# Decoded tokens next to the chain over chunks, a group's end in a lane of its own, and operations held back in program order

## The chip, the core and the metric

The kernel runs on one core of one Trainium2 chip. A core has five engines with queues of their own: TensorE (PE, with its weight loads shown as PEld), VectorE (DVE), ScalarE (ACT), GpSimd (POOL) and SyncE (SP), which here only issues transfers. The metric is the device time of one execution in microseconds (us), as a median over runs. Before the change it is 1681.28 us (three runs, 1680.93 to 1681.66).

## What is computed

One trunk layer of a hybrid causal decoder, for 256 prompt tokens and for 8 sequences of 4 decoded tokens each. All weights and states are in float32. Cut to what matters, the reference is

```python
h = rmsnorm(x, norm_pre_mix)
z = h @ w_in                                   # 2048 -> 3360 + 1024 + 2048 + 2048
zs, zp, zga, zgb = split(z)
ya, new_wkv  = rwkv7(zs + (prev(zs) - zs) * mu_shift, state_wkv, ...)   # 16 heads of 64
yb, new_pool = pool(zp, state_pool, ...)       # causal means over 2, 4, 8, 16 tokens
m = sigmoid(zga) * (ya @ w_branch_a) + sigmoid(zgb) * (yb @ w_branch_b)
x = x + rmsnorm(m @ w_out, norm_post_mix)
f, new_conv = conv_ffn(rmsnorm(x, norm_pre_ffn), state_conv, ...)       # 2048 -> 2 x 5632 -> 2048
x = x + rmsnorm(f, norm_post_ffn)
```

and the recurrence within `rwkv7`, for each head and token, with a matrix state `s` of 64 x 64:

```python
sa = s @ a_t
s = s * w_t[None, :] + outer(sa, b_t) + outer(v_t, k_t)
y_t = s @ r_t
```

followed by a normalisation of `y` over each head, a bonus term and a gate `g`.

## The kernel before, in words

**Layout.** Channels lie on the 128 partitions and the 288 tokens (256 prompt tokens and 32 decoded ones, `N`) along the free dimension. Each product of the layer goes by tiles of 128 output channels: `dense` runs over 16 (or 8, or up to 16) tiles of 128 input channels and sums them in one PSUM bank of 128 x 288.

**Weights in two parts.** Every float32 weight is split into a high part `whi` (a cast on ScalarE, L196) and the rest `wlo` (a subtraction on VectorE, L197), and every input likewise, so that three matmuls (`three`, L254 to L256) stand for one float32 product. Weights come in *units* of four input tiles (128 x 512 elements, 256 KB): `load_to` issues the load of a unit on SP, `split_to` its two casts. `take(u)` casts three units ahead and loads nine ahead. One unit is twelve dense matmuls.

**Lanes.** The side work (everything of the recurrence, the norms) is written as generators in lanes. At the end of each unit `advance` runs the operations put off by `defer` and steps each lane once, so a `yield` in a generator is a slot of one unit. `yield 2` is two slots, `yield lambda: ...` waits until the condition holds. `drain_side` steps the lanes without any dense work until they are empty.

**Order.** The mixer runs in the order of `ORDER`: r, k and v of head group 0 (two heads' tiles, 4 heads); the eight tiles of the pooling branch with `pool_product`s; group 1; 16 products of branch b; group 2; 6 gates for b; group 3; 10 gates for b; 15 gates for a. Then come the 16 products of branch a (`seq_ba`), `w_out`, and the feed-forward part in three thirds. From the end of group 0's r, k and v to the first product of branch a there are 264 units.

**One head group.** `rkv(g)` makes r, k, v and puts `front(g)` into lane 1 and `late(g)` into lane 2.

- `front(g)`: decay, its running product, and the operands `AR` and `KB` of the chunked form; it sets `ready[g]`. Then the bonus `bv`.
- `late(g)`: the products `ps_g` of 64-token chunks (L625) and their masked copy `Gm`; the transposes `ps_t` into `BK`; `ps_v` into `UV`; the diagonal 32 x 32 blocks of `Gm` go through DRAM (`dA`) into `Ab`. Then two generators step together, one step of each per slot: `inverse`, 31 pairs of a multiplication and a sum on VectorE (L782, L785) that solve the 32 x 32 triangular blocks, and `sample`, the decoded tokens: `ps_sg` (L707 to L715), five dependent steps `ps_sl` (L743) and VectorE `UVs` (L745), and the state update `ps_st` (L765). The inverse goes through DRAM (`dW`) into `W`; `dve.transpose` makes `tq` (L827), `ps_q` (L833) and `ps_w` (L845) complete the 64 x 64 inverse. Then the chain over the four chunks, three slots a chunk: `ps_x`, a copy `X`; `ps_u`, the scaling into `UV`; `ps_s` and `ps_y`, the new state `S` and the copy into `Yt` (L900). Last the end of the group: the head norm, `ps_yt` (L926), the gate products `ps_gate` (L937) and `ya`, eight tiles in all for four groups, which branch a reads.

`late(g + 1)` can only begin when `late(g)` is through, since they share lane 2. The scratch `inv` of the inverse lies in a pool (`k2`) whose memory is the pooling stage's until that is over, so group 0 waits for it (`yield lambda: k2`).

**Who orders what.** The kernel is built with a planner: it takes the instructions of each engine in the order in which they were written, but lets one that its own timing thinks ready pass others that it thinks are not. On the chip each engine runs its list in that order and waits at each instruction for its inputs. `tc.keep_in_program_order(i)` (`pin`) ties an instruction behind the one that was written last before it on its engine.

## Time and profile before

| what | before |
|---|---|
| median of three runs | 1681.28 us |
| the profiled execution | 1685.43 us |
| span of its instructions | 1683.4 us |
| mean granted TensorE clock | 0.991 |
| PE, DVE, ACT, POOL busy | 97%, 66%, 48%, 22% |
| weights and states read from HBM | 262.67 MB |

The page of the profile covers one execution. A row of its groups of instructions reads: line, engine, operation, output <- inputs, shape, count, then busy time in us and the mean of one in ns, then the idle time of the engine just before them and what ended it. Matmuls are pipelined: a row of one shows 0.29 us though the next begins 0.13 us after it, so the rate is read from starts, not from durations.

The stages by time, from the first and last products of each: the start to 77 us (norm, the low-rank columns, group 0), the mixer from 77 to 662 us, branch a from 661.6 to 712.4 us, `w_out` to about 815 us, the second norm to about 835 us, and the feed-forward part to 1667 us.

### The profile page before, as it was taken

How to read it: one execution, taken by the hardware profiler on the slowest of the kernel's cores; microseconds unless marked ns; L12 is line 12 of the kernel's file. 1: busy time of each engine (PE TensorE's matmuls, PEld its weight loads, DVE VectorE, ACT ScalarE, POOL GpSimd, SP SyncE). 2: the span in 40 equal slices, each digit the busy share in tenths (PEclk: the TensorE clock that was granted, in tenths of full speed). 3: DMA queues.
4: the chain of work that ended last, by engine and by line, in shares of the span. 5: the costliest groups of instructions: out<-in, count | busy, mean ns of one | idle time of the engine just before them, and what ended most of it. 6: DMA issues, size and time to landing. Idle time of an engine off the chain costs nothing.

```text
span 1683.4 us, 35698 instructions
## 1 busy us (share of the span) xinstructions
PE 1641.2 (97%) x13398; PEld 1594.4 (95%) x13398; DVE 1116.4 (66%) x2192; ACT 813.2 (48%) x1492; POOL 376.6 (22%) x629
## 2 busy tenths in 40 slices
PE   7999999999999999999899999999999999999998
PEld 6989889889989899999799999999999999999997
DVE  6798976977976846754786665446666655566654
ACT  6544354344444445555565554445554433455554
POOL 4584343334342201400221110001111100011112
PEclk9999999999999999999899999999999999999999
DMA  7535454444455457854355555555555565555563
GB/s 247 161 115 184 154 171 150 153 145 145 146 157 171 147 158 245 256 171 164 101 174 165 167 166 168 165 168 165 168 166 167 165 167 165 167 165 167 174 168 107
DMA packets 158125, 278.95 MB, mean 166 GB/s; under 512 B 26608, under 2 KB 33264, under 8 KB 157952
## 3 DMA queue, kind: packets, MB, share of 16 engines
q1 hardware_dynamic: 152256, 259.65, 49.5%
q0 software_dynamic: 5408, 16.27, 2.7%
q8 instruction: 105, 1.72, 0.4%
q10 hardware_dynamic: 288, 0.74, 0.1%
q14 instruction: 68, 0.56, 0.1%
HBM read 262.67 MB, written 13.93 MB: 164 GB/s over the span
## 4 chain that ended last, share of the span: by engine, by line
PE 86%; DVE 7%; DMA 2%; issue 2%; POOL 1%; ACT 0%; SPq 0%; DVEq 0%; POOLq 0%; ACTq 0%
PE acc L256 27%; PE acc L254 27%; PE acc L255 26%; DVE wlo L197 2%; DVE wt L782 1%; PE ps_g L625 1%; DVE wt L785 1%; DMA dW<-wt 1%; DMA W<-dW 0%; DMA Ab<-dA 0%; PE ps_s L881 0%; DVE AR L570 0%; PE ps_y L896 0%; PE ps_n L521 0%; PE ps_u L871 0%
## 5 line engine op out<-in xcount | busy, mean ns | idle before, releaser
L197 DVE TENSOR_TENSOR wlo<-raw,whi 128x512 fp32r<-128x512 f32 x928 | 658.8, 713 | 440.9 <-ACT whi L196 429.5
L196 ACT CAST whi<-raw 128x512 fp32r<-128x512 f32 x928 | 571.1, 619 | 663.2 <-PE acc L255 618.8
L254 PE MATMUL acc<-xh,whi 128*128 128x288 f32 x2736 | 815.2, 299 | 16.4 <-ACT whi L196 11.7
L256 PE MATMUL acc<-xh,wlo 128*128 128x288 f32 x2736 | 812.0, 297 | 6.0 <-DVE wlo L197 6.0
L255 PE MATMUL acc<-xl,whi 128*128 128x288 f32 x2736 | 812.4, 297 | 0.0
L254 PEld LDWEIGHTS acc<-xh,whi 128*128 128x128 f32 x2736 | 516.4, 189 | 23.3 <-ACT whi L196 14.0
L256 PEld LDWEIGHTS acc<-xh,wlo 128*128 128x128 f32 x2736 | 518.6, 190 | 12.4 <-DVE wlo L197 8.0
L255 PEld LDWEIGHTS acc<-xl,whi 128*128 128x128 f32 x2736 | 520.2, 190 | 2.5 <-issue 0.8
L256 PE MATMUL acc<-ah,wlo 128*128 128x288 f32 x704 | 208.7, 296 | 0.0
L254 PE MATMUL acc<-ah,whi 128*128 128x288 f32 x704 | 208.0, 296 | 0.0
L255 PE MATMUL acc<-al,whi 128*128 128x288 f32 x704 | 205.2, 292 | 0.0
L1198 POOL COPY cout<-gt 128x2 f32<-128x2 f32 x44 | 30.8, 699 | 591.8 <-DVE gt L1194 580.7
L255 PEld LDWEIGHTS acc<-al,whi 128*128 128x128 f32 x704 | 134.2, 191 | 0.0
L254 PEld LDWEIGHTS acc<-ah,whi 128*128 128x128 f32 x704 | 132.3, 188 | 0.0
L256 PEld LDWEIGHTS acc<-ah,wlo 128*128 128x128 f32 x704 | 131.9, 187 | 0.0
L782 DVE TENSOR_TENSOR wt<-wt,Ab 128x16 f32<-128x16 f32 (+30 forms) x124 | 56.8, 458 | 2.0
L1206 POOL TENSOR_TENSOR cv<-cv,rstd_ffn 128x288 f32<-128x288 f32 x44 | 36.8, 836 | 74.0 <-ACT cv L1205 73.2
L1202 DVE SCALAR_TENSOR_TENSOR cv<-gt,vec,cv 128x255 f32<-128x255 f32 x88 | 43.1, 490 | 0.0
L431 POOL TENSOR_TENSOR df<-zt 128x256 f32<-128x256 f32 (+1 forms) x27 | 21.9, 809 | 94.8 <-DVE zt L429 81.0
L256 PE MATMUL acc<-ybh,wlo 128*128 128x288 f32 x128 | 38.5, 302 | 2.6 <-DVE wlo L197 2.6
L254 PE MATMUL acc<-ybh,whi 128*128 128x288 f32 x128 | 38.4, 300 | 0.7 <-ACT whi L196 0.7
L1163 POOL TENSOR_TENSOR x<-x,og 128x288 f32<-128x288 f32 x11 | 12.9, 1170 | 114.5 <-DVE og L1162 114.5
(309 smaller groups left out, 1587.3 us busy)
## 6 DMA issues: line engine op xcount, KB each, us to landing
raw<-in_w_ffn_in SPq DMA_DIRECT2D x352, 256.0 KB, 3.0
raw<-in_w_in SPq DMA_DIRECT2D x264, 256.0 KB, 3.5
raw<-in_w_ffn_out SPq DMA_DIRECT2D x176, 256.0 KB, 2.7
raw<-in_w_out SPq DMA_DIRECT2D x64, 256.0 KB, 3.0
raw<-in_w_branch_b SPq DMA_DIRECT2D x32, 256.0 KB, 3.4
raw<-in_w_branch_a SPq DMA_DIRECT2D x32, 256.0 KB, 4.0
xr<-in_xT SPq DMA_DIRECT2D x8, 288.0 KB, 5.7
tga<-th POOLq DMA_DIRECT2D x16, 144.0 KB, 3.8
```

The source lines that it names most:

```text
L196: act.copy(out=hi[:, a:b, :m], in_=w[:, a:b, :m])
L197: dve.tensor_tensor(lo[:, a:b, :m], w[:, a:b, :m], hi[:, a:b, :m].bitcast(F32), op=ALU.subtract)
L254: pe.matmul(ps, hi, xh, start=start, stop=False)
L255: pe.matmul(ps, hi, xl, start=False, stop=False)
L256: pe.matmul(ps, lo, xh, start=False, stop=stop)
L431: pool.tensor_tensor(df[:m, :TP], zt[:m, 0:TP], zt[:m, 1:ZB], op=ALU.subtract)
L625: pe.matmul(pss[par][:, dc * G + i, :], KB[h, c, i, :, :].rearrange("p s t -> p (s t)"), AR[h, :, i, c * C:(c + 1) * C], start=True, stop= ...
L782: dve.tensor_tensor(tmp[:, :, :n], Wb[:, :, :n], Ab[:, :n, tt].unsqueeze(1).to_broadcast([P, 8, n]), op=ALU.mult)
L785: dve.tensor_reduce(out=Wb[:, :, tt], in_=tmp[:, :, :n], op=ALU.add, axis=AX.X)
L1198: pool.tensor_copy(cout[:, f, 0:2], gt[:, TP - 2:TP])
L1202: dve.scalar_tensor_tensor(cv[:, s:TP], gt[:, 0:TP - s], w, cv[:, s:TP], op0=ALU.mult, op1=ALU.add)
L1206: pool.tensor_tensor(cv, cv, rst3, op=ALU.mult)
```

## The change

- `advance` is also called in the middle of a unit, as `advance(True)`, which steps lane 2 alone. A `yield` in `late` is now half a slot.
- `late` waits four half slots after `ready`; the two halves of `ps_g` are two half slots apart, and its other waits are stretched likewise.
- `inverse` runs alone, in steps of one or two pairs (`IWORK` 300 for 800), right behind the load of `Ab`. Its scratch `inv` is in `kp`, so that it does not wait for the end of the pooling stage. The loads of `W` are issued right behind it.
- `chain` and `sample` step together, one step of each every three half slots (`STEP`). `sample` has fewer waits of its own.
- The end of a group (`finish`) goes into a third lane.
- Pinned are now: `kkr`, the casts of `rh`, `ga_h`, `gb_s` and `ya`, the copies `Xs` and `Yt`, the gates' `tanh` (ScalarE); `ps_g`, `ps_sg`, `ps_sl`, `ps_st`, `ps_q` (TensorE); the diagonal of `Ab` and the transposes into `tq` (VectorE). The gates' `tanh` and what follows it are put off by a slot.
- The pooling history is loaded by a transfer that POOL issues, straight into `zb`, where SP loaded `phist` and POOL copied it. `d` has one buffer for two.
- The first five products of branch a are begun ahead of `drain_side`, with the first four input tiles (`ya` of groups 0 and 1); their second halves follow behind it.

```diff
-IWAIT = 2
-IWORK = 800
-WWAIT = 5
+BT = 5
+IWAIT = 3
+IWORK = 300
+STEP = 3
+WWAIT = 6
...
-    seq_ba = [add_units(t["w_branch_a"][j], 8) for j in range(16)]
+    seq_ba = add_together([t["w_branch_a"][j] for j in range(BT)], 8)
+    seq_ba += [add_units(t["w_branch_a"][j], 8) for j in range(BT, 16)]
...
-    def advance():
+    def advance(half=False):
+        if half:
+            lane2.step()
+            return
         for e in later:
...
-    lane1, lane2 = Lane(), Lane()
+    lane1, lane2, lane3 = Lane(), Lane(), Lane()
...
             if j % 4 == 3 or j == nk - 1:
                 advance()
+            elif j % 4 == 1:
+                advance(True)
...
-    def exact_parts(h, l, src):
-        act.copy(out=h, in_=src)
+    def exact_parts(h, l, src, held=False):
+        i = act.copy(out=h, in_=src)
+        if held:
+            pin(i)
         dve.tensor_tensor(l, src, h.bitcast(F32), op=ALU.subtract)
...
     def late(g):
         yield lambda: g in ready
+        yield 4
...
-                    pe.matmul(
+                    pin(pe.matmul(
                         pss[par][:, dc * G + i, :],
...
-            yield
+            yield 2
...
+        def inverse():
+            yield 2 * IWAIT
+            pin(dve.memset(Ab.rearrange("p a b -> p (a b)")[:, 0:1024:33], 1.0))
+            wt = kp.tile([P, 2, 8, 32], F32, tag="inv", name="wt")
...
+        yield from inverse()
...
         yield lambda: k2
...
-        smp, inv = sample(), inverse()
-        busy = True
-        while busy:
-            busy = False
-            for e in (inv, smp):
...
-        yield WWAIT
...
+        smp = sample()
+        next(smp)
+        yield 2 * WWAIT + (0 if g else 16)
+        tq = kp.tile([P, 2, NC2, 32], F32, tag="inv", name="tq")
         Td, QT = tq[:, 0], tq[:, 1]
         for par in range(2):
-            dve.transpose(out=Td[arow(par, 0)], in_=W[arow(par, 0), :, 0:32])
-        yield
+            pin(dve.transpose(out=Td[arow(par, 0)], in_=W[arow(par, 0), :, 0:32]))
+        yield 3
...
+        run = [chain(), smp]
+        while run:
+            for e in list(run):
+                try:
+                    next(e)
+                except StopIteration:
+                    run.remove(e)
+            yield STEP
...
+        lane3.todo.append(finish())
...
-        phist = pp.tile([P, HIST * NB], F32, tag="phist", name="phist")
-        nc.sync.dma_start(out=phist, in_=t["st_pool"][:, m, :])
         zb = pp.tile([P, ZW], F32, tag="zb", name="zb")
         pool.memset(zb[:, 0:PZ], 0.0)
-        pool.tensor_copy(zb[:, SZ:SZ + HIST * NB], phist)
+        pool.dma_start(out=zb[:, SZ:SZ + HIST * NB], in_=t["st_pool"][:, m, :])
...
-        act.activation(out=th, in_=th, func=AF.Tanh, scale=0.5)
-        return th
+
+        def tanh():
+            pin(act.activation(out=th, in_=th, func=AF.Tanh, scale=0.5))
+            then(th)
+
+        defer(tanh, 1)
...
+    pba = [p.tile([P, 512], F32, tag=tag, name="acc") for p, tag in [(psa, "acc")] * 3 + [(psg, "g")] * 2]
+    for j in range(BT):
+        dense_unit(pba[j], seq_ba[j][0], yah, yal, 0, 8)
     drain_side()
```

More of the change, by code (lines that the diff above doesn't have):

```diff
@@ L345, in hybrid_step @@
     TC = N // 3
-    pin = tc.keep_in_program_order
     def rstd_spread(sums, where, between=()):
@@ L719, in sample @@
             Xs = kp.tile([P, G, C], F32, tag="Xs", name="Xs")
-            act.copy(out=Xs, in_=ps[:, 2])
+            pin(act.copy(out=Xs, in_=ps[:, 2]))
             for i in range(G):
@@ L742, in sample @@
                     h = HALF[par]
-                    pe.matmul(psl[h, i], Gs[h, i], src[h, i], start=True, stop=True)
+                    pin(pe.matmul(psl[h, i], Gs[h, i], src[h, i], start=True, stop=True))
                 if s < NS:
@@ L764, in sample @@
                     h = HALF[par]
-                    pe.matmul(pst[h], BKs[h, i], uxs[i][h], start=True, stop=True)
+                    pin(pe.matmul(pst[h], BKs[h, i], uxs[i][h], start=True, stop=True))
                 psts.append(pst)
@@ L794, in late @@
-        smp, inv = sample(), inverse()
-        busy = True
-        while busy:
-            busy = False
-            for e in (inv, smp):
-                try:
-                    next(e)
-                    busy = True
-                except StopIteration:
-                    pass
-            if busy:
-                yield
-        low = kp.tile([P, 2, G * P], F32, tag="Ab", name="low")
-        g2a, g2b = low[:, 0], low[0:96, 1]
-        nc.sync.dma_start(out=g2a, in_=t["g2a"][:, gc])
@@ L931, in late @@
-        yield
-        for i in range(G):
-            m = p0 + i
-            ms = slice(i * P, (i + 1) * P)
-            ps = psb.tile([P, 512], F32, tag="s", name="ps_gate")
-            three(ps[:, :N], ga_h[:, ms], ga_l[:, ms], zg0_h, zg0_l, True, False)
-            pe.matmul(ps[:, :N], gb_s[:, ms], zg1_s, start=False, stop=True)
-            dve.tensor_tensor(Yc[:, i], Yc[:, i], ps[:, :N], op=ALU.mult)
-            ya[m] = y_parts(m, "ya")
-            exact_parts(*ya[m], Yc[:, i])
-        yield
+        yield 3
@@ new lines, in late @@
+        run = [chain(), smp]
[6 more added lines that the diff above has]
+            yield STEP
+        S = state[0]
+        pool.dma_start(out=t["o_pwkv"][:, p0:p0 + G, :], in_=S)
+        ga_h, ga_l = (kp.tile([P, G * P], F32R, tag=n, name=n) for n in ("ga_h", "ga_l"))
+        gb_s = kp.tile([96, G * P], F32R, tag="gb_s", name="gb_s")
+        exact_parts(ga_h, ga_l, g2a, True)
@@ new lines, in late, with finish @@
+        pin(act.copy(out=gb_s, in_=g2b))
+        dve.tensor_tensor(gb_s[64:96], g2b[64:96], gb_s[64:96].bitcast(F32), op=ALU.subtract)
+        def finish():
+            NY = NC2 + G
+            st = kp.tile([P, NY, 1], F32, tag="st", name="st")
+            dve.tensor_reduce(out=st, in_=Yt, op=ALU.add, axis=AX.X)
+            dve.tensor_scalar(st, st, 1.0 / C, None, op0=ALU.mult)
+            dve.tensor_tensor(Yt, Yt, st.to_broadcast([P, NY, C]), op=ALU.subtract)
+            q2 = kp.tile([P, NY, C], F32, tag="BK", name="q2")
+            act.activation(out=q2, in_=Yt, func=AF.Square)
+            yield
+            dve.tensor_reduce(out=st, in_=q2, op=ALU.add, axis=AX.X)
+            act.activation(out=st, in_=st, func=AF.Sqrt, scale=1.0 / C, bias=c_("gneps"))
+            dve.reciprocal(st, st)
+            dve.tensor_tensor(Yt, Yt, st.to_broadcast([P, NY, C]), op=ALU.mult)
+            yield 2
+            Yc = k2[0].tile(W2, F32, tag="Yc", name="Yc")
+            for i in range(G):
+                m = p0 + i
+                ps = psb.tile([P, 512], F32, tag="s", name="ps_yt")
+                for c in range(NCH):
+                    for par in range(2):
+                        h = HALF[par]
+                        pe.matmul(ps[h, c * C:(c + 1) * C], Yt[h, c * G + i, :], ident[h, h], start=True, stop=True)
+                for par in range(2):
+                    h, r = HALF[par], slice(64 * par, 64 * par + 32)
+                    pe.matmul(ps[h, TP:N], Yt[r, NC2 + i, :], ident[r, r], start=True, stop=True, tile_position=(h.start, h.start))
+                dve.scalar_tensor_tensor(Yc[:, i], ps[:, :N], v_("lw", m), bvs.pop((g, i)), op0=ALU.mult, op1=ALU.add)
+            yield
+            for i in range(G):
+                m = p0 + i
+                ms = slice(i * P, (i + 1) * P)
+                ps = psb.tile([P, 512], F32, tag="s", name="ps_gate")
+                three(ps[:, :N], ga_h[:, ms], ga_l[:, ms], zg0_h, zg0_l, True, False)
+                pe.matmul(ps[:, :N], gb_s[:, ms], zg1_s, start=False, stop=True)
+                dve.tensor_tensor(Yc[:, i], Yc[:, i], ps[:, :N], op=ALU.mult)
+                yield
+                ya[m] = y_parts(m, "ya")
+                exact_parts(*ya[m], Yc[:, i], True)
@@ L1103, in hybrid_step @@
         fetch(j + FA)
-        ps = dense(seq_ba[j], yah, yal)
+        if j < BT:
+            ps = pba[j]
+            dense_unit(ps, seq_ba[j][1], yah, yal, 4, 8)
+        else:
+            ps = dense(seq_ba[j], yah, yal)
         th, mb = tin[j]
```

233 lines of the change are left out of this document (100 added, 133 removed).

## The prediction

> **What bounds the kernel now.** I read the page first, then the busy time by stretch, then TensorE's waits inside the mixer, then TensorE's own timeline around its small products. The page:
>
> ```profile
> span 1683.4 us, 35698 instructions
> PE 1641.2 (97%) x13398; PEld 1594.4 (95%) x13398; DVE 1116.4 (66%) x2192; ACT 813.2 (48%) x1492; POOL 376.6 (22%) x629
> PE 86%; DVE 7%; DMA 2%; issue 2%; POOL 1%; ACT 0%; SPq 0%; DVEq 0%; POOLq 0%; ACTq 0%
> ```
>
> TensorE sets the time: 86% of the chain that ended last. The profiled execution took 1685.43 us for this span; the median of the runs shown is 1681.28 us, 4.15 us less. I make the sum as a difference and subtract it from both. Busy time by stretch (columns: stretch and length, then busy us and instructions of PE, PEld, DVE, ACT and POOL, the granted clock, DMA share, GB/s):
>
> ```profile
> 77.00:662.00 585.00, 568.30 (x5416) 528.36 (x5415) 451.19 (x977) 260.31 (x506) 211.55 (x365) 0.99 0.50 156
> 100.00:110.00 10.00, 8.52 (x47) 8.33 (x48) 9.79 (x16) 2.46 (x4) 9.77 (x17) 0.66 0.37 116
> 380.00:390.00 10.00, 10.00 (x77) 8.82 (x76) 5.35 (x12) 3.40 (x7) 2.18 (x5) 0.66 0.42 136
> 107.00:157.00 50.00, 50.00 (x406) 48.57 (x406) 39.27 (x86) 24.69 (x48) 27.34 (x50) 0.99 0.56 173
> 157.00:203.00 46.00, 46.00 (x406) 42.92 (x405) 44.72 (x115) 18.07 (x34) 18.93 (x38) 1.00 0.43 144
> 860.00:1660.00 800.00, 800.00 (x6052) 800.00 (x6051) 469.72 (x884) 398.04 (x683) 84.46 (x145) 1.00 0.54 166
> ```
>
> The last row is the pure dense rate: 800 us / 6052 = 0.132 us for a matmul, 1.59 us for a weight unit of twelve. The feed-forward part stands at that rate and the change doesn't touch it. All that it touches lies in the first row, the mixer, where 264 units (a slot each: 585 / 264 = 2.2 us) carry the side work of four head groups. There TensorE stands idle 585 - 568.3 = 16.7 us, and in two stretches of 10 us its granted clock is 0.66, which is 3.4 us lost in each. TensorE's waits in that stretch (us in total, times, longest):
>
> ```profile
> PE ps_g L625 <- DVE AR L570: 5.4, 3, 3.3
> PE ps_q L833 <- DVE tq L827: 3.8, 5, 1.5
> PE acc L256 <- DVE wlo L197: 3.6, 7, 1.1
> PE acc L254 <- ACT whi L196: 2.3, 3, 1.2
> PE ps_sl L743 <- DVE Gs L722: 1.0, 2, 0.8
> PE ps_s L881 <- DVE UV L874: 0.3, 1, 0.3
> ```
>
> They come to 16.4 us: all of the idle time has a name. The rest of what side work costs is paid in trips: TensorE leaves the dense stream for a few small products and comes back. Two trips, by start and duration of each row:
>
> ```profile
> 170.57 0.29 PE L256 MATMUL acc<-xh,wlo 128*128 128x288 f32 x1
> 170.79 0.45 PE L743 MATMUL ps_sl<-UV,Gs 64*64 64x64 f32 x8
> 171.17 0.40 PE L254 MATMUL acc<-xh,whi 128*128 128x288 f32 x1
> 171.41 0.29 PE L255 MATMUL acc<-xl,whi 128*128 128x288 f32 x1
> ...
> 235.45 0.29 PE L254 MATMUL acc<-ybh,whi 128*128 128x288 f32 x1
> 235.67 0.34 PE L860 MATMUL ps_x<-S,AR 64*64 64x64 f32 x4
> ...
> 236.33 0.40 PE L255 MATMUL acc<-ybl,whi 128*128 128x288 f32 x1
> 236.57 0.29 PE L256 MATMUL acc<-ybh,wlo 128*128 128x288 f32 x1
> ```
>
> From the dense start ahead of the trip to the second dense start behind it, the trip with eight products takes 171.41 - 170.57 = 0.84 us, where two dense periods would take 0.26: price 0.58 us. The trip with sixteen takes 1.12 us, price 0.86. So two trips of eight joined in one save 2 x 0.58 - 0.86 = 0.30 us.
>
> **Part 1, decoded tokens beside the chain.** Before, the decode steps run next to the inverse, each ps_sl in a slot without other side products. After, one step of the chain over chunks and one decode step are issued in the same half slot, and the decode matmuls are pinned behind the chain's. So ps_sg joins the first ps_x, the five ps_sl join ps_y, ps_x, ps_u, ps_y, ps_x, and ps_st the last ps_x. The counts:
>
> ```profile
> L743 PE MATMUL ps_sl<-UVs,Gs x128: 218/218/267, 174.5 to 571.0; 64*64 64x64 f32 x128
> L743 PE MATMUL ps_sl<-UV,Gs x32: 218/218/267, 170.8 to 555.6; 64*64 64x64 f32 x32
> ...
> 314.52 1.08 PE ps_st L765 x4
> 316.45 1.01 PE ps_st L765 x4
> ```
>
> 160 ps_sl products are 20 trips of eight; ps_st and ps_sg give 4 joins each: 28 x 0.30 = 8.4 us. Against it, ps_g is now pinned with a slot between its halves and no longer shares a trip with other work, as it did here:
>
> ```profile
> 101.48 3.10 PE L625 MATMUL ps_g<-AR,KB 64*128 64x128 f32 x16 [3.32 <-DVE AR L570]
> 104.51 1.97 PE L653 MATMUL ps_t<-con,KB 128*128 128x128 f32 x8
> ...
> 378.76 1.13 PE L625 MATMUL ps_g<-AR,KB 64*128 64x128 f32 x8 [1.64 <-DVE AR L570]
> ```
>
> I take one such trip more in each group, 4 x 0.30 = 1.2 us. **Part 1: -7.2 us**; bounds 0 (nothing joins, because UVs on VectorE comes late) and -8.4.
>
> **Part 2, held operations.** A pin puts an instruction behind what was written before it on its engine; without one the planner puts it where its own timing thinks it ready. It helps only where the written place lies later than the true readiness. I counted slots from the yields.
> *ps_g waiting for AR.* For group 0 the written place moves from slot 10 to slot 12. But the row at 101.48 already stood behind the twelfth unit of the pooling stage, so the 3.3 us stay, with their 3.4 us of clock. For group 2 the written place is about 130 against an observed 133, no hold either, but all that runs beside it is arranged anew. Of the other 5.4 - 3.3 = 2.1 us and the second 3.4 us I take half: -2.7; bounds 0 and -12.2 (5.4 + 2 x 3.4). The rows show the clock low behind a wait of 3.32 us and behind one of 1.64.
> [...]
> *ps_q waiting for tq.* The transposes wait for W, whose load waits for the inverse. Its cost:
>
> ```profile
> L782 DVE TENSOR_TENSOR wt<-wt,Ab 128x16 f32<-128x16 f32 (+30 forms) x124 | 56.8, 458 | 2.0
> L785 DVE TENSOR_REDUCE wt<-wt 128x8 f32<-128x16 f32 (+30 forms) x124 | 36.2, 292 | 1.9
> ...
> L782 DVE TENSOR_TENSOR wt<-wt,Ab x31: 164/423/990, 159.2 to 202.3; 128x16 f32<-128x16 f32 x1, 128x24 f32<-128x24 f32 x1, 128x32 f32<-128x32 f32 x1, 128x40 f32<-128x40 f32 x1
> ```
>
> (56.8 + 36.2) / 4 = 23.3 us of VectorE in each group. In group 0 (last row, its first and last start) it was spread over 43 us, 20 slots. The new program writes it into 13 slots and holds the transposes 6 more, 19 in all (27 for group 0). So the hold is about as long as the inverse; half of 3.8, -1.9; bounds 0 and -3.8.
> *wlo and whi late.* ScalarE's pinned casts (kkr, rh, Yt, ga_h, the gates' tanh, ya) no longer stand in front of a weight cast while they wait. A waiting ACT or DVE holds up the casts behind it, and the dense products behind these; three units are cast ahead, 4.8 us of cover. Half of 3.6 + 2.3: -3.0; bounds 0 and -5.9. Gs and UV (1.3 us): decode matmuls pinned one and a half slots apart can wait as easily, with the dense products queued behind them; 0, bounds -1.3 and, if each of twenty ps_sl waited the 0.5 us of the two seen, +10. **Part 2: -7.6 us**; bounds +10 and -23.2 (16.4 + 6.8).
>
> **Part 3, the inverse of group 0 moves into the pooling stage.** Its scratch no longer waits for the pooling stage's memory, so slots 19 to 32 carry it, about 107 to 157 us. There VectorE has 50 - 39.3 = 10.7 us free, and 23.3 come: 12.6 us too much. In the row 157 to 203 VectorE was 97% busy with the same inverse and PE 46.00 of 46: the planner stretched the inverse and let the weight casts pass. I expect that again, at 2 us for d and dl of the pooling products, due one slot after they are made. Bounds 0 and +12.6.
> [...]
>
> **Part 4, what costs nothing.** The pooling history comes by a POOL-issued transfer instead of an SP load and a POOL copy:
>
> ```profile
> L976 POOL COPY zb<-phist x8: 286/532/702, 20.9 to 139.8; 128x120 f32<-128x120 f32 x8
> tga<-th POOLq DMA_DIRECT2D x16, 144.0 KB, 3.8
> phist<-in_st_pool SPq DMA_DIRECT2D x8, 60.0 KB, 3.6
> ```
>
> The copy's 0.53 us of POOL goes, an issue comes, and the landing takes as long from either queue. Uncovered, POOL would stand up to 3.6 us in each of eight tiles with the window sums queued behind it; the pooling products follow four slots (8.8 us) later. The first halves of five branch-a products are the same 60 matmuls in another order. Their outputs then come one unit apart, 1.59 us, for which POOL has
>
> ```profile
> L1107 POOL TENSOR_TENSOR tga<-tga,mb 128x288 f32<-128x288 f32 x16 | 19.6, 1225 | 29.2 <-ACT whi L196 16.9 <-DVE tga L1106 6.3 <-DMA raw<-in_w_branch_a 4.0
> ```
>
> 1.225 us: it fits. The finish in its own lane removes 5 slots from each group's turn, and the half slots of the chain (19.5 slots where 12 were written) add more. What must hold is the end:
>
> ```profile
> L937 PE MATMUL ps_gate<-zg_s,gb_s x8: 295/298/302, 282.1 to 652.5; 96*128 96x288 f32 x8
> L254 PE MATMUL acc<-yah,whi x128: 293/295/298, 661.6 to 712.0; 128*128 128x288 f32 x128
> ```
>
> Before, the last ps_gate came 9.1 us, 4 slots, before branch a needs it, though it was written at slot 233 of 264: the true run lags the written one by about 27 slots. After, it is written at slot 241. With the same lag that is 268, inside the five units (to 269) now placed in front of the drain. I expect a smaller lag, since the chain is written with 4.5 slots a chunk and no longer 3, and the inverse has VectorE without the decode steps: cost 0.
>
> **Sum.** -7.2 - 7.6 + 2 = -12.8 us. The profiled execution goes from 1685.4 to 1672.6, the median from 1681.3 to **1668.5 us**.
>
> **The rivals.**
> *All waits go.* If every hold comes late enough, part 2 is 23.2 us and part 1 stays: 1681.3 - 7.2 - 23.2 = 1650.9. For it: every wait named in the table has an instruction that is now pinned or behind one. Against it: the slot counts, by which AR is not held beyond its readiness.
> *The holds don't hold and the trips don't join.* The true run lags the written one by up to 27 slots, so the planner may ignore most written places; then 1681.3, within 0.2% (3.4 us, what a measurement of this kernel can tell from no change).
> *The pooling stage starves (slower).* The 12.6 us of surplus VectorE work fall on TensorE, if d, dl and wlo stand behind the inverse, in two waits over 1.6 us that cost 3.4 us of clock each: +19.4 in place of +2, and the waits of part 2 stay since VectorE runs late into the next stage: 1681.3 - 7.2 + 19.4 = 1693.5. It decides from the point where a pooling product waits for dl. For it: VectorE is 9.79 of 10 busy at 100 to 110 already. Against it: the 46.00 of 46.
> *Group 3 ends too late (slower).* If the lag grows by 10 slots, the end lies at 278, 9 slots behind the cover, with nothing dense beside it: 9 x 2.2 = 19.8; 1668.5 + 19.8 = 1688.3. For it: 52.5 slots a group against 49. Against it: the chain at its true pace, and the decode steps out of the inverse.
>
> **How the numbers follow.** Forecast 57% (own range 1659 to 1677: part 1 and part 2 between half and one and a half), all waits go 13%, no change 12%, pooling starves 10%, late end 8%. From 1655 to 1688 lies the forecast with no change and most of the late ends, and a part of the first rival; about 2 in 10 are left out, at both ends together. Faster takes the forecast, the first rival and 2 points of the late ends: 0.72; same the no-change case less a fringe of 1: 0.11; slower the rest: 0.17.
>
> **What would show it.** Right: trips in which ps_sl follows ps_x, ps_u or ps_y without a dense product between; ps_q's wait under 2 us; the first AR wait still there with a clock of 0.66 behind it; the inverse of group 0 between 107 and 170 us with PE full; the last ps_gate ahead of the first yah product of the second halves. Wrong: ps_sl trips alone (part 1 gone), a wait of acc for dl or wlo between 107 and 170 (pooling starves), a gap with no dense product ahead of branch a's second halves, or new waits of ps_sl or ps_sg in place of the old ones.

## The result and the profile after

The changed kernel takes 1666.57 us (median of four runs, 1662.20 to 1670.99). Its ratio to the kernel before is **0.9897**, with a 95% interval of 0.9874 to 0.9920: faster by 1.0%. On the 1681.28 us of before that is 17.3 us less (13.5 to 21.2); the medians alone differ by 14.7 us. The forecast was 1668.5 us, by a sum of 12.8 us: the direction is right and the size somewhat short. The profiled execution took 1666.09 us, where that of before took 1685.43.

The page of the profile after, span, busy time and the chain that ended last:

```profile
span 1664.3 us, 35679 instructions
PE 1627.8 (98%) x13398; PEld 1589.1 (95%) x13398; DVE 1104.5 (66%) x2192; ACT 814.6 (49%) x1492; POOL 382.0 (23%) x629
PE 88%; DVE 5%; POOL 2%; DMA 2%; issue 1%; ACT 0%; SPq 0%; DVEq 0%; POOLq 0%
```

TensorE does the same 13398 products and is busy 13.4 us less. TensorE's waits in the mixer (us in total, times, longest), to be read against the six rows of before:

```profile
PE ps_g L637 <- DVE AR L581: 5.4, 2, 3.3
PE ps_q L826 <- DVE tq L820: 2.7, 4, 1.7
PE acc L260 <- ACT dh L343: 0.9, 1, 0.9
PE acc L261 <- DVE dl L346: 0.9, 1, 0.9
PE acc L262 <- DVE wlo L200: 0.7, 1, 0.7
PE ps_g L637 <- POOL KB L595: 0.3, 1, 0.3
PE acc L260 <- DVE th L1060: 0.2, 1, 0.2
```

The seven rows come to 11.1 us where the six of before came to 16.4 (shorter ones bring both to 11.4 and 16.7). The waits for AR are as long as they were, `whi` and `Gs` are gone, `dh` and `dl` are new. Busy time by stretch (length, then busy us and instructions of PE, PEld, DVE, ACT, POOL, the granted clock, DMA share, GB/s):

```profile
100.00:110.00 10.00, 7.89 (x41) 7.09 (x42) 9.85 (x14) 0.62 (x1) 9.56 (x16) 0.66 0.39 112
107.00:157.00 50.00, 48.27 (x392) 47.14 (x391) 44.11 (x118) 25.63 (x49) 28.97 (x50) 0.99 0.54 167
350.00:360.00 10.00, 10.00 (x116) 9.05 (x115) 7.74 (x21) 4.11 (x9) 3.73 (x7) 0.87 0.37 120
450.00:460.00 10.00, 10.00 (x165) 9.62 (x164) 3.24 (x9) 4.60 (x13) 3.12 (x4) 0.85 0.47 148
480.00:490.00 10.00, 7.88 (x77) 7.37 (x76) 9.94 (x14) 3.03 (x6) 9.01 (x10) 0.86 0.16 53
```

In place of two stretches at 0.66 there is one, at 100 us behind the first wait for AR, and three at 0.85 to 0.87. Three joined trips in TensorE's timeline (start and duration of each row):

```profile
205.03 0.29 PE L262 MATMUL acc<-ybh,wlo 128*128 128x288 f32 x1
205.25 0.34 PE L856 MATMUL ps_x<-S,AR 64*64 64x64 f32 x4
...
205.77 0.23 PE L786 MATMUL ps_sl<-UVs,Gs 64*64 64x64 f32 x2
205.92 0.40 PE L260 MATMUL acc<-ybh,whi 128*128 128x288 f32 x1
206.16 0.29 PE L261 MATMUL acc<-ybl,whi 128*128 128x288 f32 x1
...
208.44 0.29 PE L260 MATMUL acc<-ybh,whi 128*128 128x288 f32 x1
208.67 0.45 PE L867 MATMUL ps_u<-X,W 64*64 64x64 f32 x8
208.95 0.40 PE L786 MATMUL ps_sl<-UVs,Gs 64*64 64x64 f32 x8
209.28 0.40 PE L261 MATMUL acc<-ybl,whi 128*128 128x288 f32 x1
209.51 0.29 PE L262 MATMUL acc<-ybh,wlo 128*128 128x288 f32 x1
...
241.04 0.29 PE L260 MATMUL acc<-ybh,whi 128*128 128x288 f32 x1
...
242.05 1.45 PE L807 MATMUL ps_st<-ux,BKs 64*64 64x512 f32 x6
243.43 0.40 PE L261 MATMUL acc<-ybl,whi 128*128 128x288 f32 x1
243.67 0.29 PE L262 MATMUL acc<-ybh,wlo 128*128 128x288 f32 x1
```

By the prediction's measure (first dense start ahead to second dense start behind, less 0.26 us) `ps_x` with `ps_sl`, 24 products, costs 0.87 us, where `ps_x` alone, 16 products, cost 0.86. `ps_u` with `ps_sl` costs 0.81, the trip of eight `ps_st` with `ps_x` 2.37.

For the comparison of all kernels below I divide the mixer, from TensorE's 433rd dense product to its 4033rd, by the starts of successive products: its 3600 dense products at the pure rate (476.3 us in every kernel), waits, trips (by the same measure as above: from the dense start ahead of small products to the second dense start behind them, less two dense periods and the waits), and the rest, which is dense time above the pure rate; in the mixer the granted clock is 0.50 over 13.7 us before and over 17.1 us in the changed kernel. All in us, each from one profiled execution, which need not be a typical one: that of e6 is 4.5 us above its median, that of e8 5.4 us above, that of e3 6.1 us below.

| kernel | mixer | waits | trips (count) | rest | ratio to before, 95% interval |
|---|---|---|---|---|---|
| before | 636.7 | 16.7 | 137.4 (123) | 6.3 | 1 |
| changed | 617.1 | 11.4 | 122.2 (93) | 7.2 | 0.9897 [0.9874, 0.9920] |
| e1_apart | 620.5 | 16.0 | 121.4 (93) | 6.8 | 0.9898 [0.9873, 0.9922] |
| e3_decode_free | 614.1 | 12.6 | 120.3 (93) | 5.0 | 0.9905 [0.9881, 0.9930] |
| e2_no_pins | 619.8 | 12.8 | 123.8 (92) | 7.0 | 0.9903 [0.9881, 0.9925] |
| e5_no_first_halves | 619.3 | 14.7 | 121.6 (93) | 6.7 | 0.9914 [0.9899, 0.9930] |
| e10_joins_and_order_only | 620.4 | 14.0 | 124.9 (92) | 5.3 | 0.9919 [0.9890, 0.9949] |
| e4_hold_g0 | 623.3 | 15.4 | 121.4 (91) | 10.1 | 0.9923 [0.9901, 0.9946] |
| e6_inverse_after_pool | 632.4 | 19.7 | 122.6 (95) | 13.9 | 0.9968 [0.9956, 0.9980] |
| e7_decode_in_inverse | 635.7 | 18.2 | 129.8 (111) | 11.4 | 0.9996 [0.9982, 1.0010] |
| e8_side_by_side_alone | 642.1 | 27.1 | 128.2 (81) | 10.5 | 0.9997 [0.9981, 1.0013] |
| e9_pins_alone | 644.3 | 19.4 | 136.9 (125) | 11.7 | 1.0032 [1.0019, 1.0046] |

From before to the changed kernel the mixer loses 19.6 us: 15.2 in trips, 5.3 in waits, and 0.9 come back as rest. The rows of e1 and e3 turn out to be the changed program again; over these three executions trips fall by 15.2 to 17.1 us and waits by 0.7 to 5.3. Outside it nothing moved: the time ahead of the mixer is 75.7 us before and 76.0 after, the time behind it 971.0 and 971.2.

### The profile page after: what moved, and what is told of

The parts are those of the page before. It is cut to its first block, busy times and chain, and to the rows that moved or that the text cites. A ratio compares the mean times of both kernels' runs of the same rounds, so it can differ in the third digit from the quotient of the medians.

```text
span 1664.3 us, 35679 instructions
## 1 busy us (share of the span) xinstructions
PE 1627.8 (98%) x13398; PEld 1589.1 (95%) x13398; DVE 1104.5 (66%) x2192; ACT 814.6 (49%) x1492; POOL 382.0 (23%) x629
## 3 DMA queue, kind: packets, MB, share of 16 engines
q8 instruction: 105, 1.72, 0.4%
## 4 chain that ended last, share of the span: by engine, by line
PE 88%; DVE 5%; POOL 2%; DMA 2%; issue 1%; ACT 0%; SPq 0%; DVEq 0%; POOLq 0%
PE acc L262 27%; PE acc L260 27%; PE acc L261 27%; DVE wlo L200 1%; DVE wt L699 1%; DMA dW<-wt 1%; PE ps_g L637 1%; DVE wt L702 0%; PE ps_sg L759 0%; POOL win L998 0%; PE ps_s L877 0%; DMA W<-dW 0%; PE ps_st L807 0%; PE ps_y L892 0%; PE ps_u L867 0%
## 5 line engine op out<-in xcount | busy, mean ns | idle before, releaser
L699 DVE TENSOR_TENSOR wt<-wt,Ab 128x16 f32<-128x16 f32 (+30 forms) x124 | 52.6, 425 | 1.3
```

The costliest lines, as they stand in the source:

```text
L699: dve.tensor_tensor(tmp[:, :, :n], Wb[:, :, :n], Ab[:, :n, tt].unsqueeze(1).to_broadcast([P, 8, n]), op=ALU.mult)
```

## The experiments

Four readings were open. *Trips*: joining decode and chain is the gain. *Holds*: the pins and the later written places are the gain, or a part of it. *VectorE's backlog*: the waits come from work queued on VectorE, wherever a waiting product is written. *Late end*: what the other edits do is to let group 3 end beside the gate products. The expectations use letters for them (J the trips, H and P the holds, D the backlog, L the joins with the room that a late end needs); where one gives a letter another meaning it says so in place. Each kernel is the changed one with the edit shown, except e8 and e9, which start from the kernel before. Ratios and the division of the mixer are in the table above.

### The joins taken apart by half a unit: e1_apart, and decode unpinned: e3_decode_free

```diff
             for e in list(run):
                 try:
                     next(e)
...
-            yield STEP
+                n += 1
+                yield
+            yield STEP - n
```

> The changed kernel with one thing undone: the chain's step and the decode step are still issued at the same pace (one of each every three half slots) and still pinned, but half a unit apart, so that six dense matmuls stand between them. Theory J (joined trips are the larger part of the gain): the 28 joins come apart, 0.30 to 0.39 us each, so the time rises by 8 to 11 us over the changed kernel, to about 1675 to 1678 us or a ratio of about 0.997 to kernel before; the count of trips goes from 93 back to about 120; the waits stay as they are. Rival P (the pins and holds made the gain): within 3 us of the changed kernel, ratio 0.988 to 0.992.

```diff
-                    pin(pe.matmul(psl[h, i], Gs[h, i], src[h, i], start=True, stop=True))
+                    free(pe.matmul(psl[h, i], Gs[h, i], src[h, i], start=True, stop=True))
...
-                    pin(pe.matmul(pst[h], BKs[h, i], uxs[i][h], start=True, stop=True))
+                    free(pe.matmul(pst[h], BKs[h, i], uxs[i][h], start=True, stop=True))
```

> The changed kernel without the pins on the decode products alone (ps_sg, ps_sl, ps_st); all other pins stay. If the joins hang on these pins, the trips go up from 93 towards 120 and the time by 4 to 9 us. If being written side by side is enough, the trips stay near 93 and the time within 2 us of the changed kernel.

Measured: 1668.76 us (0.9898) and 1670.07 us (0.9905). Neither edit undid anything. The planner puts out the same list of instructions, on all five engines, as for the changed kernel: a step written half a unit later still lands in the same trip, and the decode products stand in the same places without their pins. So these two runs say nothing on trips against holds. They are the changed kernel taken twice more, and show its spread. The waits of e1_apart, the same list as after:

```profile
PE ps_g L637 <- DVE AR L581: 7.9, 3, 4.3
```

Waits of 11.4, 16.0 and 12.6 us, and a mixer of 617.1, 620.5 and 614.1, belong to one and the same program. A difference of 5 us in the waits of two single profiles is no finding.

### All pins removed: e2_no_pins

```diff
+    def free(i):
+        return i
...
-            pin(act.activation(out=kkr[:, i], in_=kx[:, i], func=AF.Copy, scale=v_("kk", p0 + i)))
+            free(act.activation(out=kkr[:, i], in_=kx[:, i], func=AF.Copy, scale=v_("kk", p0 + i)))
...
-                    pin(pe.matmul(
+                    free(pe.matmul(
                         pss[par][:, dc * G + i, :],
```

and likewise at all fifteen places where the change pins.

> The changed kernel without any of the new pins; order, slots, half slots and joins are as written. Theory J: the decode products, no longer tied behind the chain's, go where the planner thinks them ready, so some joins come apart (0 to 8 us), and waits for tq, wlo and whi come back (up to 5 us): +3 to +10 us over the changed kernel. Rival P: all of the gain is lost, about 1681 us. Rival S (the slots alone do it, the pins are idle): within 2 us of the changed kernel.

Measured: 1669.44 us, 0.9903 [0.9881, 0.9925]; 92 trips, waits 12.8 us. The pins are idle for the time. They are not idle in the profile. ScalarE's waits in the mixer, first of the kernel before, then of the changed kernel, then without the pins:

```profile
ACT ga_h L333 <- DMA low<-in_g2a: 17.3, 4, 5.9
ACT kkr L500 <- DVE kx L439: 16.1, 6, 3.8
ACT rh L333 <- DVE rr L580: 13.4, 4, 4.7
```

```profile
ACT rh L343 <- DVE rr L591: 2.5, 1, 2.5
```

```profile
ACT ga_h L346 <- DMA low<-in_g2a: 10.7, 4, 3.2
ACT kkr L514 <- DVE kx L453: 7.7, 5, 2.2
ACT rh L346 <- DVE rr L594: 6.5, 2, 4.7
ACT rh L346 <- DVE AR L584: 6.0, 2, 3.8
```

ScalarE stood in front of these three casts for 46.8 us before and 2.5 after: just what the prediction says a hold does. Without the pins 30.9 us of it return, and TensorE does not notice: its waits for `whi` are none in either kernel, those for `wlo` 0.2 us here and 0.7 in the changed kernel. Not every hold shortens ScalarE's waits: the gates' `tanh` (tile `th`) waits 17.3 us with its pin and 9.3 without. Nor is the cover of three units complete: in e10_joins_and_order_only below, also without pins, TensorE waits 1.7 us for `whi`, at 318.6 and 445.9 us, behind two `ga_h` casts that had waited 2.6 and 2.5 us for their load.

### The pins alone: e9_pins_alone

The kernel before, with the same pins and the gates' `tanh` put off by a slot; all other order and slots as before.

```diff
-        exact_parts(ga_h, ga_l, g2a)
-        act.copy(out=gb_s, in_=g2b)
+        exact_parts(ga_h, ga_l, g2a, True)
+        pin(act.copy(out=gb_s, in_=g2b))
...
-        act.activation(out=th, in_=th, func=AF.Tanh, scale=0.5)
-        return th
+        def tanh():
+            pin(act.activation(out=th, in_=th, func=AF.Tanh, scale=0.5))
+            then(th)
+
+        defer(tanh, 1)
```

> The kernel before with the new pins alone (the same 15 places, and the gates' tanh put off by a slot); slots, lanes and order are those of before. Theory: the pins hold nothing that the planner does not hold by itself, trips stay at about 123, waits near 16 us: ratio 0.998 to 1.002. Rival P (the pins take the waits away): waits of 5 to 9 us for 16.4, ratio 0.993 to 0.996.

Measured: 1691.28 us, 1.0032 [1.0019, 1.0046], slower, and above both expectations. ScalarE's timeline ahead of TensorE's longest new wait:

```profile
462.39 0.45 ACT L1053 ACTIVATE th<-th 128x288 f32<-128x288 f32 x1 [3.50 <-DVE th L1050]
467.81 0.40 ACT L335 CAST ga_h<-low 128x256 fp32r<-128x256 f32 x1 [4.97 <-DMA low<-in_g2a]
468.12 0.61 ACT L196 CAST whi<-raw 128x512 fp32r<-128x512 f32 x1
```

and the wait itself, in TensorE's waits:

```profile
PE acc L254 <- ACT whi L196: 5.1, 3, 3.8
```

The pinned `tanh` waits 3.50 us, the pinned cast of `ga_h` 4.97 us for its load, a weight cast stands behind them, and the cover is used up: TensorE waits 3.84 us at 468.8. The pin did not make this stall: without it the four `ga_h` casts of before wait 17.3 us for their loads, here 18.3, and before, too, TensorE's three waits for `whi` end at 209.0, 336.2 and 464.9 us, 1 to 2 us behind the start of such a cast. In the changed kernel the cast is written behind the chain, long after its load, and with its pin waits for nothing. A pin at a place that is too early doesn't help; why this kernel is slower than the one before, and how much of it is the pins and how much the later `tanh`, isn't shown.

### A later written place for group 0's first products: e4_hold_g0

```diff
-        yield 4
+        yield 4 if g else 12
```

> The changed kernel, with ps_g of group 0 held four slots longer (12 half slots for 4); group 0 waits for the pooling stage's memory anyway, so nothing behind it moves. Theory H (the wait for AR is a matter of the written place): the 3.3 us of wait at 98 us and the 3.4 us of low clock behind it go, -5 to -7 us, about 1660 us. Rival D (VectorE is full there, 9.85 of 10 us busy, and is the bound): the wait moves to dl or wlo in the same place, 0 to -2 us.

Measured: 1672.88 us, 0.9923 [0.9901, 0.9946]. TensorE's waits, and the stretch from 100 to 110 us:

```profile
PE acc L261 <- DVE dl L346: 6.4, 2, 5.6
...
PE ps_g L637 <- DVE AR L581: 1.8, 1, 1.8
```

```profile
100.00:110.00 10.00, 4.98 (x19) 4.66 (x20) 8.45 (x12) 0.62 (x1) 9.70 (x16) 0.54 0.39 107
```

Neither number was met: it is not faster than the changed kernel, and the intervals overlap. The 3.3 us in front of `ps_g` at 98 us are gone, and a dense product waits 5.6 us for `dl` in the same place. Against the expectation something behind it moved as well: group 0's inverse begins at 141.2 us for 134.1. VectorE is the bound there: AR, KB, the pooling's own sums and the weight rests are queued on it, and with `ps_g` out of the way TensorE runs into the next of them. The first wait for AR is no matter of where `ps_g` is written.

### No first halves of branch a: e5_no_first_halves

```diff
-BT = 5
+BT = 0
```

> The changed kernel with the first halves of branch a taken out again (BT = 0): all 16 products of branch a follow the drain, as before. Theory (they cover nothing here): the last ps_gate of group 3 still ends ahead of branch a, so the time stays within 2 us of the changed kernel, ratio 0.988 to 0.992. Rival (late end: the five units cover group 3's end): a stretch without dense products ahead of branch a, up to five units, +8 us, ratio about 0.994.

Measured: 1669.04 us, 0.9914 [0.9899, 0.9930]. Group 3 ends in time without cover (its last `ps_gate` starts 7.5 us ahead of branch a here too), so the five first halves cover nothing. In the changed kernel, the rows of the gate products of the groups and of branch a (first and last start behind the durations):

```profile
L950 PE MATMUL ps_gate<-zg_s,gb_s x8: 295/298/300, 266.9 to 634.8; 96*128 96x288 f32 x8
...
L260 PE MATMUL acc<-yah,whi x128: 293/295/298, 642.3 to 692.7; 128*128 128x288 f32 x128
```

Group 3's last `ps_gate` starts at 634.8 us, branch a at 642.3: the end is 7.5 us early, as it was 9.1 us early before the change, and the first halves only follow then.

### Group 0's inverse behind the pooling stage again: e6_inverse_after_pool

```diff
+        yield lambda: k2
         yield from inverse()
...
-        yield 2 * WWAIT + (0 if g else 16)
+        yield 2 * WWAIT
```

> The changed kernel with group 0's inverse put back behind the pooling stage (as before the change), and without the 16 half slots that only group 0 waits. Theory L (the early inverse buys the time by which group 3 ends): the waits of TensorE for dh and dl between 138 and 158 us (about 2 us) go, but all four groups end about 8 slots later, and the last ps_gate falls about seven units behind the start of branch a: two units or more without dense work, +3 to +12 us, ratio 0.993 to 0.997. Rival D (the early inverse only crowds VectorE): 2 us less than the changed kernel.

Measured: 1678.44 us, 0.9968 [0.9956, 0.9980]. Two thirds of the gain are lost, with the trips as in the changed kernel. Group 3 does end late. The last of these rows, and what TensorE did meanwhile:

```profile
L951 PE MATMUL ps_gate<-zg_s,gb_s x8: 295/298/300, 292.9 to 663.7; 96*128 96x288 f32 x8
```

```profile
240.00:250.00 10.00, 7.20 (x54) 6.31 (x54) 9.47 (x16) 2.88 (x7) 6.14 (x8) 0.66 0.39 128
...
638.00:664.00 26.00, 26.00 (x261) 23.02 (x260) 15.71 (x29) 10.31 (x19) 2.70 (x5) 1.00 0.45 147
```

Branch a begins at 648.4 us and group 3 ends at 664.0, 15.6 us later, but TensorE is busy 26.00 of 26 us around it, at full clock: 84 products of branch a run ahead of the last `ps_gate`, the first halves among them, so there is no stretch without dense work. The time falls in the range of theory L, but not by its price. The loss lies in the waits and what follows them:

```profile
PE acc L262 <- DVE wlo L200: 4.4, 3, 2.8
...
PE ps_sl L787 <- DVE UVs L789: 3.5, 2, 2.5
```

The later inverse pushes group 0's chain and decode into the time of group 1's `front`; at 244 us `ps_sl` waits 2.46 us for `UVs`, with 9.47 of 10 us of VectorE taken, and the clock is 0.66 in that stretch. At 460 us it is `wlo`, 2.8 us. Behind the late end, at 679 us, branch a waits 3.0 us for `tga`, with a granted clock of 0.83 from 680 to 690 us after it; in the changed kernel branch a waits for nothing, so this may be a cost of the late end after all. Waits and rest are 8.3 and 6.7 us above the changed kernel's, and above those of its two repeats.

### Decode beside the inverse again, in groups 1 to 3: e7_decode_in_inverse

```diff
-        yield from inverse()
...
+        n = 0
+        for _ in inverse():
+            for w in range(_ or 1):
+                n += 1
+                if smp and n % 3 == 0:
+                    next(smp, None)
+                yield
```

For groups 1 to 3 `sample` is set up ahead of the inverse (not shown). Group 0's inverse stays early and alone, and its decode stays with the chain; pins, half slots, lane and first halves stay.

> The changed kernel with the decode steps of groups 1 to 3 put back next to the inverse (one step every three half slots) and the chain alone behind it; group 0 keeps them next to the chain. Pins, half slots, the finish lane and the early inverse stay. Theory J (joined trips are the larger part of the gain): 18 trips more (111 for 93 in the mixer) at 0.39 to 0.51 us of edges and of products within trips, +7 to +9 us over the changed kernel, ratio 0.994 to 0.995. Rival S (the finer slots and the early inverse made the gain): within 2 us of the changed kernel, ratio 0.989 to 0.991.

Measured: 1683.49 us, 0.9996 [0.9982, 1.0010]: the whole gain is gone, with one part undone in three groups of four. The trips rise by 18 and cost 7.6 us more, as theory J has it; waits rise by 6.8 and the rest by 4.2 us, which is more than half of the 18.6 us. Against the other two executions of the changed program waits rise by 2.2 and 5.6 us, so this part is less certain than the trips. TensorE's waits:

```profile
PE ps_q L838 <- DVE tq L832: 5.9, 5, 2.3
...
PE ps_sl L743 <- DVE Gs L724: 2.9, 2, 1.9
```

With decode beside it, the inverse shares VectorE with `Gs` and `UVs`, and `Gs` is waited for; in none of the three executions of the changed program is it. For `tq` TensorE waits 5.9 us, against 2.7, 4.2 and 3.0 in those three. So the part that the prediction priced by its trips alone also takes the wait for `Gs` off the path, and perhaps a part of that for `tq`.

### Part 1 alone: e8_side_by_side_alone

The kernel before; each group's inverse runs by itself, then chain and decode together, one step of each per slot, with fewer waits in `sample` (not shown). No pins, half slots, third lane or early inverse.

```diff
-        smp, inv = sample(), inverse()
-        busy = True
-        while busy:
...
+        yield from inverse()
...
+        run = [chain(), smp]
+        while run:
+            for e in list(run):
...
+            if run:
+                yield
```

> The kernel before with part 1 alone: each group's inverse runs by itself, then its chain over chunks and its decoded tokens together, one step of each per slot; no pins, no half slots, no first group ahead in the pooling stage, no lane of its own for a group's end. In the built order TensorE leaves the dense products 87 times (123 before, 93 in the changed kernel), but group 3's whole chain, decode and end, some 67 such departures' worth of rows, stand behind the last of the gate products. Theory L (the joins gain by the trip, and the other edits are there so that group 3 still ends beside the gate products): the trips' share of the mixer falls by 9 to 15 us, and group 3's end stands uncovered behind the gate products, by several tens of us; the sum is slower than before, above 1700. Rival T (the joins alone are the change, the rest is idle): faster than before by about what the changed kernel is, 1666 to 1673, with group 3's end filled in by other work.

Measured: 1685.06 us, 0.9997 [0.9981, 1.0013]: no change, between the two expectations and met by neither. The joins are there: in groups 0 to 2 no decode product has a trip of its own. The count of 81 trips is low also because most of group 3's work is one trip. That part of group 3 stands behind the gate products, which end at 627.9 us: from 637.5 to 667.1 us it runs with nothing dense beside it, behind 54 products of branch a. The longest wait in TensorE's timeline there:

```profile
662.00 1.12 PE L928 MATMUL ps_yt<-con,Yt 64*64 64x64 f32 x16 [5.92 <-DVE Yt L918]
```

I had put the price of this at several tens of us beyond the gain. It is less, since the tail is one trip of 29.6 us of which 9.3 us are waits; the rest are products that have to be done anyway and save the returns to the dense stream. The change of the sum, in the slowest of its ten executions: trips -9.2, waits +10.4 (of which 9.3 in the tail), rest +4.2.

### Joins and order without pins and first halves: e10_joins_and_order_only

```diff
-BT = 5
+BT = 0
...
-                    pin(pe.matmul(
+                    free(pe.matmul(
```

(and `free` at all fifteen places, as in e2_no_pins).

> The changed kernel without any of its new pins and without the five first halves of branch a; what remains is the joins, the early inverse, the half slots, the lane for a group's end and the transfer by POOL. Theory L (the joins pay, and the order of the group makes room for them; pins and first halves are idle): 1666 to 1671, as the changed kernel, with 90 to 95 trips and the last ps_gate within 2 us of the end of the gate products. Rival H (pins and first halves stand in for each other, so that each alone could go for nothing but both together not): 1675 or more, with the end of group 3 behind the gate products by several us or waits of over 18 us.

Measured: 1669.62 us, 0.9919 [0.9890, 0.9949], 92 trips, the last `ps_gate` through at 638.2 us and branch a from 645.5, so group 3 ends 7 us early, more than the 2 us that the first expectation had. What is left of the change is as fast as the whole of it, within the intervals. No version that was run beats the changed kernel. The half slots, the third lane, the finer steps of the inverse and the transfer by POOL were never taken out alone, so what each of them is worth stays open.

## Why the prediction was right, and where it was not

**The sum.** It was -12.8 us against -17.3 (-13.5 to -21.2) by the ratio, -14.7 by the medians and -19.3 in the profiled pair. The sign, the 57% case and the place (all in the mixer, nothing behind it) were right. The terms were less right than their sum: part 1 was too small, and part 2 came out near its size by another cause than the one given, which is luck.

**Part 1 was mis-sized: -7.2 us said, -15.2 measured in the trips.** The step that failed is "two trips of eight joined in one save 2 x 0.58 - 0.86 = 0.30 us". It took the trip of sixteen `ps_x` products as the price of any joined trip. For two trips of eight that comes near: `ps_u` with `ps_sl` costs 0.81. But eight of the twenty `ps_sl` trips join that very trip of sixteen, and the joins with `ps_st` and `ps_sg` are larger ones. By pairs, as means over such trips, from the starts of TensorE's products:

- `ps_sl` joined to `ps_x` saves 0.58 + 0.86 - 0.87 = 0.57 us, eight times: 4.6 us;
- to `ps_u`, whose trip alone also costs 0.58, 0.58 + 0.58 - 0.81 = 0.35, four times: 1.4 us;
- to `ps_s` and `ps_y`, 0.58 + 0.81 - 1.19 or 0.58 + 1.34 - 1.72, so 0.20, eight times: 1.6 us;
- `ps_st` had two trips of 1.2 us in groups 1 to 3 (the rows at 314.52 and 316.45) and one of 2.06 in group 0, and has now one with `ps_x`: 2.4 + 0.86 - 2.37 = 0.9, three times, and 0.55: 3.2 us;
- `ps_sg` with `ps_w`, `ps_x` and `ps_u` is one trip of 3.97 us where there were three of 2.67, 1.58 and 0.58: 0.86, four times if groups 0 and 1 are taken like 2 and 3: 3.4 us.

That is 14.2 us. `ps_g` standing alone costs 0.61 + 1.28 for 1.55, three times, so 1.0 us for the 1.2 said. Of the 2.0 us that are left, 1.05 lie in one trip of `ps_s` and `ps_y` before the change, which cost 2.39 us at 383 us, in the stretch with the clock of 0.66, where others cost 1.34; the rest lies in other trips. All of it together is beyond the bound of -8.4 that the prediction set. By this list some 35 trips went into others, where 28 joins were said; the count fell by 30, since others, `ps_g` among them, were split. Why eight more products cost `ps_x` only 0.01 us isn't shown; the rows show `ps_sl` between `ps_x` products, two at a time. One difference in the code is isolated by no run: `ps_x` reads one half of the partitions and writes the other, while `ps_sl` and `ps_u`, which share a trip less cheaply, each read and write the same half.

**Part 1 also had a second half that was not priced.** e7 shows that undoing it costs waits for `Gs` and `tq` (8.8 us together, for 2.7 to 4.2 in the three executions of the changed program) and clock (0.68 from 320 to 330 us, 0.83 in three other stretches of 10 us), not trips alone. The prediction named the inverse "without the decode steps" only for the end of group 3.

**Part 2 gave about the right number by a cause that falls.** Waits fell by 5.3 us net of the 2 new ones. By its terms: AR was to lose 1.0 us of wait and 1.7 of clock, and lost nothing (5.4 and 5.4; the rest rose from 6.3 to 7.2); `tq` -1.1 where -1.9 was said; `wlo` and `whi` -5.2 where -3.0 was said; `Gs` and `UV` -1.3 where 0 was said. The step that failed is that ScalarE's pinned casts "no longer stand in front of a weight cast while they wait". Three of them no longer do, the `tanh` still does; e2 has the three waiting again at no price, and e9 has the pins without the new places at a loss of 0.3%. So most of what took `whi` and `wlo` away is the new order: they come to 5.9 us before and 6.5 with the pins alone (e9), and to 0.2 (e2) and 2.3 (e10) with the new order and no pins, for 0.7 with both. The 2.3 leave room for a share of the holds. Which edit of the order it is, is not settled, since the waits of one program differ by 4.6 us between executions. That also means that the -5.3 itself is hardly more than the spread.

**The first wait for AR stayed**, with 0.66 behind it, as forecast, since the row "already stood behind the twelfth unit of the pooling stage". e4 shows the deeper reason: VectorE is late there, and with `ps_g` out of the way the next product in line waits instead. A part of that may be GpSimd's. AR's four operations take 0.87 to 1.81 us before:

```profile
L570 DVE SCALAR_TENSOR_TENSOR AR<-kkr,thw x4: 870/1549/1814, 99.5 to 495.2; 128x576 f32<-128x576 f32 x4
```

Each of them ends 0.61 to 0.62 us behind the end of the GpSimd operation that runs when it begins (the first, from 99.52 us, beside a `KB` operation of 1.70 us from 99.01); in the changed kernel all four do so too, at 0.62 us. By this the first one may have stood for 1.81 - 0.62 = 1.2 us, an estimate from these times alone; no run was made for it.

**Part 3 was right as a cost and incomplete as a step.** The new waits are `dh` 0.9, `dl` 0.9 and `th` 0.2, 2.0 us, for 2 forecast; TensorE was busy 48.27 of 50 us between 107 and 157. The inverse stood later than said:

```profile
L699 DVE TENSOR_TENSOR wt<-wt,Ab x31: 178/497/919, 134.1 to 181.5; 128x16 f32<-128x16 f32 x1, 128x24 f32<-128x24 f32 x1, 128x32 f32<-128x32 f32 x1, 128x40 f32<-128x40 f32 x1
L699 DVE TENSOR_TENSOR wt<-wt,Ab 128x16 f32<-128x16 f32 (+30 forms) x31 | 14.5, 467 | 0.2
```

VectorE's surplus thus came later than in the slots that the prediction counted. What it left out is what this move buys: e6 puts it at 0.7% of the time, through waits and clock in group 1's `front` and later. The 31 multiplications take 14.5 us here; the same 31 take (52.6 - 14.5) / 3 = 12.7 us on average in this kernel's other three groups, and took 13.3 in group 0 before. The 1.8 us lie in four of them, of 0.61 to 0.92 us each where the other groups have 0.23 to 0.39; three of the four begin while a GpSimd operation runs and end 0.09 to 0.16 us behind its end. So they take 1.8 us more here; whether any of it reached TensorE isn't shown.

**Part 4 was right.** The pooling history lands as fast from POOL's queue (us to landing last):

```profile
zb<-in_st_pool POOLq DMA_DIRECT2D x8, 60.0 KB, 3.2
```

where the SP load took 3.6. The first halves are worth nothing here (e5). In e6 they run beside a late group 3; no run has the late end of e6 without them. The prediction put the last `ps_gate` at slot 268 by the old lag, inside their cover, and expected a smaller lag; it came 7.5 us ahead of the cover.

**The rivals.** *All waits go* (1650.9): 11.4 of 16.7 us stayed. *No change* (1681.3): the trips joined. *The pooling stage starves* (1693.5): it was to decide when a pooling product waits for `dl` over 1.6 us; the waits are 0.9 and 0.9. So its sign, a wait for `dl` between 107 and 170 us, did appear (at 142.7 us), but the sign was given without a size, and the cost was the 2 us of the forecast. *Group 3 ends too late* (1688.3): not in the changed kernel. In e8, without half slots, third lane and early inverse, the end stood uncovered for 29.6 us and took the gain of the joins.

## What to carry to other kernels

Price a joined trip by the very pair that joins, alone and together, not by a trip of like length; small products that enter a trip of sixteen can cost almost nothing (here eight `ps_sl` added 0.01 us to `ps_x`). A reorder of side work is worth what its tail allows: the same joins came with a gain of 1.0% in an order that leaves room for the last group to end, and with none in the old order, where its end stood alone. Before giving a gain to a hold, take it out alone and put it in alone: here the pins changed ScalarE's waits for three casts by some 30 us and the time by nothing that could be measured, while the old order with the pins (and a later `tanh`) was slower. One profile is one execution: run the same program again before a difference of a few us in the waits is explained.

## What the runs showed of the hardware that was not expected

The same list of instructions on the same inputs waits differently each time: 11.4, 16.0 and 12.6 us in three profiled executions, a mixer of 614.1 to 620.5 us. The low clock too comes and goes: the stretch from 350 to 360 us, in which TensorE is busy all 10 us and waits for nothing, has a granted clock of 0.87 in the changed kernel and 1.00 in e1_apart, the same program. Narrower stretches of the changed kernel show where it is low (columns as above):

```profile
354.10:357.50 3.40, 3.40 (x71) 3.00 (x69) 2.91 (x8) 1.20 (x3) 1.75 (x3) 1.00 0.44 154
357.50:360.90 3.40, 3.40 (x16) 3.40 (x15) 2.81 (x9) 0.89 (x2) 1.75 (x3) 0.50 0.00 0
```

The clock is 0.50 over the 3.4 us of the second row and 1.00 over the 3.4 us ahead of them. A stretch of 10 us that holds 2.5 us of this reads 1 - 0.5 x 2.5 / 10 = 0.87. The 0.85 from 450 to 460 us and the 0.86 from 480 to 490 us also hold a part of 3.4 us at 0.50 each, from 449.7 and from 487.2 us. The 0.66 from 380 to 390 us before is 6.8 us at 0.50, from 381.0 to 387.8 us: 1 - 0.5 x 6.8 / 10. So the values of 0.85 to 0.87, where the prediction knew only 0.66, are 3.4 us of half clock, cut by an end of the stretch, where 0.66 is 6.8 us of it.

The 3.3 us wait at 98 us has 0.66 behind it. The half clock from 357.5 us stands behind no wait over 0.2 us in that profile since 319.8 us, and TensorE is busy all 3.40 us ahead of it; but 40 of its 71 products there are `ps_n`, with two columns each, and only five dense products start, where 3.4 / 0.132 = 26 would fit. So a wait does not explain this row. Few dense products alone don't either: from 579.4 to 582.8 us in the same profile two of them start, and the clock is 1.00 there and in the 3.4 us behind. What decides it is open, and no run here was made for it.
